# A chunked RWKV-7 recurrence on one core: odd heads keep the halves of their factors in opposite order

## The chip, the core and the metric

The program runs on one core of a Trainium2 chip. The metric is the device time of one execution in microseconds (us); lower is better. The core has a matrix engine (TensorE, PE below), a vector engine (VectorE, DVE), a scalar engine (ScalarE, ACT), GpSimd (POOL) and SyncE (SP), which here issues nearly all DMA transfers. They run at the same time and wait for each other by semaphores; each takes its own instructions in order.

## What is computed

One inference step of a decoder layer, for 2048 prompt tokens and 64 sample tokens (8 sequences of 8), in fp32 with width 1024. Token mixing has two parallel groups behind one input projection: sliding-window attention and RWKV-7 time mixing with 8 heads of 64. Then come an output projection and a gated convolutional feed-forward layer. The change touches the RWKV-7 recurrence, which the reference gives token by token:

```
def step(S, inp):
    r_t, w_t, k_t, v_t, kk_t, a_t = inp
    sa = jnp.einsum('bhij,bhj->bhi', S, kk_t)
    S = (S * w_t[:, :, None, :] - sa[..., None] * (kk_t * a_t)[:, :, None, :]
         + v_t[..., None] * k_t[:, :, None, :])
    return S, jnp.einsum('bhij,bhj->bhi', S, r_t)

S_T, ys = lax.scan(step, s0.astype(f32), xs)
```

## The kernel before

**Two kinds of work.** The dense stream (`Dense`) runs the projections P, the output projections O and the feed-forward stages F over five groups of up to 448 tokens (the last has 320). Each weight tile `w` is split into a rounded half `wh` (cast on ACT, L349) and a remainder `wl` (DVE, L350), and each product takes three float32r matmuls: `wh` with `xhi`, `wh` with `xlo`, `wl` with `xhi`. They are called gm, and pf in the second half of the feed-forward layer. The mixer (`Mixer`) runs attention and the recurrence in 8 units of 256 tokens, and one unit for the sample tokens, as generators that yield between steps.

**The recurrence in chunks.** A chunk is 64 tokens; a unit has 4, the prompt 32. The projection stage leaves for each pair of heads two factors in a DRAM tensor `ab`: `ar` (128 columns: 64 of the removal factor a, 64 of the receptance r) and `bk` (64 of b, 64 of k). Partitions 0 to 63 belong to the even head of the pair, 64 to 127 to the odd one. Per chunk:

- `scores` multiplies bk by ar into G, 128 x 128 for each head: tiles sc_e (even heads, array rows 0 to 63) and sc_o (odd heads, rows 64 to 127). A mask is applied on DVE.
- `invert` inverts the unit-triangular 64 x 64 corner of each G by 32 x 32 blocks. The diagonal blocks of a unit's heads go through DRAM (dgr) to one partition each, are inverted there by 31 steps on DVE, and come back (dxr, dtr). Two rounds of eight small matmuls (pz) join the blocks.
- `chain` walks over the chunks in order. `solve` sums into pr the part of G that acts on the values and the part of the entering state S, copies it (rhs), multiplies by the inverse (pu) and copies the result, negated, into the upper half of uv. Then pS updates S for the next chunk, and `outputs` adds state part and G part into py, which is copied to y after every second chunk.

In `solve` each head's matmul uses the same corner of the array: G's rows 64 to 127 and output partitions 0 to 63 for pr, rows 0 to 63 and the same partitions for pu.

**What sets the order.** `Clock` adds up an estimated PE time per matmul. `Flow` lets the dense stream run and, by that clock, steps the mixer's generators in windows of the dense stream; a unit may use at most its share of `UNIT` (62e3 ns) in its window. A tile framework then orders the instructions of each engine by priority and gives out buffers, so that a matmul waits for the copy that empties its buffer. The mixer has five PSUM banks: three with the tag "a" and two with the tag "o", which attention's po and the recurrence's py use.

Of the kernel before, what the change touches and what calls it, by code (L numbers as in the profile page):

```python
# [80 lines left out]
class Shared:  # L81
# [13 lines left out]
    def load(self, eng, *names):  # L95
        shapes = {"vec": [128, NV], "ident": [128, 128], "ones": [128, 128], "sel": [128, 32], "blockones": [128, 128],
                  "wkmask": [128, 128], "amask": [128, 256], "sink": [128, 8], "g_up": [96, 512], "smask": [128, 128],
                  "samask": [128, 160], "ssink": [128, 2], "sshift": [128, 14, 8], "gT": [128, 3 * KT], "cw": [128, NF, 4],
                  "sconv": [128, NF, DB, 2]}
# [8 lines left out]
    def derived(self):  # L108
# [31 lines left out]
        for i in range(2):  # L140
            s = cp.tile([128, 4, 128], F32, name=f"S{i}")
# [31 lines left out]
class Clock:  # L173
# [115 lines left out]
UNIT = 62e3  # L289
# [21 lines left out]
class Dense:  # L311
# [331 lines left out]
    def pair(self, t0, n, segs, p, k, r, vt, st):  # L643
# [58 lines left out]
        for i, t in enumerate((ar, bk)):  # L702
            self.store(sh.ab[t0 // CH:t0 // CH + m, :, p, i, :].rearrange("c q t -> q c t"), t)
# [208 lines left out]
class Mixer:  # L912
# [26 lines left out]
    def scores(self, c, mask, Gs):  # L939
# [9 lines left out]
        m = mask.unsqueeze(1).to_broadcast([128, 4, 128])  # L949
        Gv = G.rearrange("p (q e) t -> p e q t", e=2)  # L950
        for i, ps in enumerate((pe, po)):
            nc.vector.tensor_tensor(out=Gv[:, i], in0=ps.rearrange("p (q t) -> p q t", t=128), in1=m, op=ALU.mult)
# [3 lines left out]
    def invert(self, Gs):  # L956
# [4 lines left out]
        dg = self.dp.tile([64, 1024], F32, tag="dg", name="dgr")  # L961
        for c, G in enumerate(Gs):
            for b in range(2):
                q = slice(32 * b, 32 * b + 32)
                dst = dg[16 * c + 8 * b:16 * c + 8 * b + 8, :].rearrange("h (s t) -> s h t", t=32)
                nc.sync.dma_start(out=dst, in_=G[q, :, q])
# [28 lines left out]
        for c, G in enumerate(Gs):  # L995
            for b in range(2):
                q = slice(32 * b, 32 * b + 32)
                nc.sync.dma_start(out=G[q, :, q], in_=dx[16 * c + 8 * b:16 * c + 8 * b + 8, :].rearrange("h (s t) -> s h t", t=32))
# [3 lines left out]
        for c, G in enumerate(Gs):  # L1002
# [3 lines left out]
            t11 = zt[0:32].rearrange("s (h t) -> s h t", t=32)  # L1006
            pz = self.ps("pz")
            for h in range(NH):
                te.matmul(pz[32:64, 32 * h:32 * h + 32], G[0:32, h, 32:64], t11[:, h, :], start=True, stop=True)
            nc.scalar.copy(out=zt[32:64], in_=pz[32:64, 0:256])  # L1010
            yield 2500
            pz = self.ps("pz")
            for h in range(NH):
                te.matmul(pz[0:32, 32 * h:32 * h + 32], zt[32:64, 32 * h:32 * h + 32], G[32:64, h, 32:64], start=True, stop=True)
            nc.scalar.activation(out=G[0:32, :, 32:64], in_=pz[0:32, 0:256].rearrange("p (h t) -> p h t", t=32),
                                 func=AF.Copy, scale=-1.0)
            yield 1500

    def zt(self, dt, c):
        zt = self.sp.tile([64, 256], F32, tag="zt", name="zt", bufs=2)  # L1020
        self.nc.sync.dma_start(out=zt[0:32].rearrange("s (h t) -> s h t", t=32), in_=dt[16 * c:16 * c + 8, :].rearrange("h (s t) -> s h t", t=32))
# [11 lines left out]
    def solve(self, G, uv, state):  # L1033

        nc, te = self.nc, self.te
        hq = [slice(64 * h, 64 * h + 64) for h in range(NH)]
        pr = self.ps("pr")
        for h in range(NH):
            te.matmul(pr[0:64, hq[h]], G[64:128, h, 0:64], uv[64:128, hq[h]], start=h == 0, stop=False)
        for p in range(4):  # L1040
            ls = state(p)
            for i, (l, r) in enumerate(ls):
                te.matmul(pr[0:64, 128 * p:128 * p + 128], l, r, start=False, stop=p == 3 and i == len(ls) - 1)
        rhs = self.rhs("rhs")[0:64]
        nc.scalar.copy(out=rhs, in_=pr[0:64])
        yield 2500
        pu = self.ps("pu")
        for h in range(NH):
# [4 lines left out]
    def outputs(self, py, G, uv, state):  # L1053
        te = self.te
        hq = [slice(64 * h, 64 * h + 64) for h in range(NH)]
        for p in range(4):
            for i, (l, r) in enumerate(state(p)):
                te.matmul(py[:, 128 * p:128 * p + 128], l, r, start=p == 0 and i == 0, stop=False)
        for h in range(NH):
            te.matmul(py[:, hq[h]], G[:, h, 64:128], uv[:, hq[h]], start=False, stop=h == NH - 1)  # L1060

    def chain(self, c0, Gs, ys):

        nc, v, te, sh = self.nc, self.nc.vector, self.te, self.sh
        hh = [slice(0, 64), slice(64, 128)]
# [10 lines left out]
        for c in range(NC_):  # L1076
            if c % 2 == 0:
# [3 lines left out]
                for i in range(2):  # L1081
                    uvs[c + i] = self.t2("uv", tag="uv", bufs=2)
                    nc.scalar.copy(out=uvs[c + i][64:128], in_=pv[64 * i:64 * i + 64])
# [14 lines left out]
            pS4 = pS.rearrange("q (p d) -> q p d", d=128)  # L1098
            ec = sh.EC[:, c0 + c, :].unsqueeze(2).to_broadcast([128, 4, 64])
            for q in hh:  # L1100
                v.tensor_tensor(out=Sn[q, :, q], in0=pS4[q, :, q], in1=S[q, :, q], op=ALU.add)
            for q in hh:
                v.tensor_tensor(out=Sn[q, :, q], in0=Sn[q, :, q], in1=ec[q], op=ALU.mult)
            yield 500
            if c % 2 == 0:
                py = self.ps("py", "o")
            self.outputs(y_rows(py, c), G, uv, lambda p: [(ars[p][:, 64:128], S[:, p, :])])
            if c % 2 == 1:
                y = self.t2("y", tag="y", bufs=2)
                nc.scalar.copy(out=y, in_=py)  # L1110
                ys.append(y)
# [116 lines left out]
    def unit(self, u, need):  # L1228
# [10 lines left out]
        def recurrence():  # L1239
# [9 lines left out]
            if c0 + NC_ == sh.nch:  # L1249
                for q in (slice(0, 64), slice(64, 128)):  # L1250
                    self.store(a["o_wkv"][q], sh.S[self.si][q, :, q])
# [5 lines left out]
    def sample(self, need):  # L1257
# [85 lines left out]
        nc.scalar.copy(out=uv[64:128], in_=pv[0:64])  # L1343
# [3 lines left out]
        def entering(x, ps, first, last):  # L1347

            s0 = self.state(0) if x else nxt
            for p in range(4):  # L1350
                am = self.rhs("am", (DB, 64))
                v.tensor_tensor(out=am, in0=ars[p][:, x:x + 64].unsqueeze(1).to_broadcast([128, DB, 64]), in1=bm, op=ALU.mult)
                s1 = self.state(p + 1) if p < 3 else None
                yield 4000
                for b in range(DB):
                    te.matmul(ps[0:64, 128 * p:128 * p + 128], am[:, b, :], s0[:, b, :], start=first and not p and not b,
                              stop=last and p == 3 and b == DB - 1)
                s0 = s1

        pr = self.ps("pr")  # L1360
        for h in range(NH):
# [246 lines left out]
```

## Time and profile before

| | |
|---|---|
| time, median of 3 runs | 2988.53 us (2986.6 to 2989.17) |
| the profiled execution | 2993.85 us, span 2992.1 us |
| mean granted PE clock in it | 0.977 of full speed |
| PE busy | 2845.7 us, 95% |
| DVE busy | 1964.8 us, 66% |
| ACT busy | 1371.4 us, 46% |

The profile is of one execution. Busy time of PE is modelled from its pipelined matmuls, so 95% says that PE seldom idles, not that the array is full. An fp32 matmul shows as two matmuls in the trace, a float32r matmul as one.

### The profile page before, as it was taken

The page shows a single profiled execution, that of the slowest core. Times are in us where ns is not written, and L with a number is a line of the kernel's source. Part 1 is how long each engine was busy: PE and PEld are TensorE (multiplying, and loading weights), DVE is VectorE, ACT ScalarE, POOL GpSimd, SP SyncE. Part 2 cuts the span into 40 slices and gives each one's busy share as a digit, 9 for nine tenths or more (in the row PEclk, how much of TensorE's full clock was granted, in tenths as well). Part 3 has the DMA queues.
Part 4 walks back from the last instruction along what each step waited for, and adds up shares of the span by engine and source line. Part 5 has one row for each costly group of instructions (what it writes and reads, how often), then busy time and mean ns, then how long its engine had stood idle before and what let it go on. Part 6 is the DMA issues. An engine that isn't in the chain of part 4 may idle for free.

```text
span 2992.1 us, 45465 instructions
## 1 busy us (share of the span) xinstructions
PE 2845.7 (95%) x16737; PEld 2447.9 (82%) x16737; DVE 1964.8 (66%) x3862; ACT 1371.4 (46%) x2430; POOL 270.8 (9%) x531
## 2 busy tenths in 40 slices
PE   6999999989999998889999997999999999998997
PEld 4877777768878997678889885999878888997997
DVE  5787776776573546866835577455588676458566
ACT  5465453545454343555533344434455442344443
POOL 0011010000000000220100000000000011001111
PEclk9999999999999999999999998999999999999998
DMA  6675546646433345555433345433347434346443
GB/s 195 191 214 180 158 126 211 195 143 209 128 121 119 115 129 161 185 164 157 130 117 118 113 151 179 135 109 116 118 124 234 135 114 123 109 130 209 149 148 116
DMA packets 302654, 447.50 MB, mean 150 GB/s; under 512 B 94024, under 2 KB 232552, under 8 KB 302416
## 3 DMA queue, kind: packets, MB, share of 16 engines
q1 hardware_dynamic: 302000, 444.45, 47.8%
q8 instruction: 132, 2.16, 0.3%
q14 instruction: 90, 0.74, 0.1%
q10 hardware_dynamic: 432, 0.16, 0.0%
HBM read 363.18 MB, written 76.97 MB: 147 GB/s over the span
## 4 chain that ended last, share of the span: by engine, by line
PE 79%; DVE 12%; DMA 4%; ACT 2%; issue 2%; SPq 0%; DVEq 0%; POOL 0%; ACTq 0%; POOLq 0%
PE gm L182 48%; PE pf L182 15%; PE pr L182 3%; PE py L182 2%; DVE wl L350 2%; PE po L182 1%; PE pz L182 1%; PE pu L182 1%; DVE tt L984 1%; DVE tmp L983 1%; PE pS L182 1%; PE ppt L186 1%; PE sc L182 1%; PE ms L182 1%; PE sc_e L182 1%
## 5 line engine op out<-in xcount | busy, mean ns | idle before, releaser
L182 PE MATMUL gm<-xhi,wh 128*128 128x448 f32 (+3 forms) x2880 | 1059.5, 369 | 31.1 <-ACT xhi L349 17.9
L182 PE MATMUL gm<-xhi,wl 128*128 128x448 f32 (+3 forms) x2880 | 1034.8, 360 | 13.4 <-DVE wl L350 13.0
L182 PE MATMUL gm<-xlo,wh 128*128 128x448 f32 (+3 forms) x2880 | 1035.5, 360 | 3.8 <-DVE xlo L350 3.5
L349 ACT CAST wh<-w 128x1024 fp32r<-128x1024 f32 (+1 forms) x470 | 489.1, 1041 | 843.6 <-PE gm L182 413.2
L350 DVE TENSOR_TENSOR wl<-w,wh 128x1024 fp32r<-128x1024 f32 (+1 forms) x470 | 570.1, 1213 | 458.8 <-ACT wh L349 452.0
L182 PEld LDWEIGHTS gm<-xhi,wh 128*128 128x128 f32 (+2 forms) x2880 | 543.4, 189 | 119.0 <-issue 32.5
L182 PEld LDWEIGHTS gm<-xhi,wl 128*128 128x128 f32 (+2 forms) x2880 | 543.6, 189 | 68.3 <-DVE wl L350 20.3
L182 PEld LDWEIGHTS gm<-xlo,wh 128*128 128x128 f32 (+2 forms) x2880 | 544.6, 189 | 56.7 <-DVE xlo L350 11.0
L182 PE MATMUL pf<-hh,wh 128*128 128x448 f32 (+1 forms) x880 | 324.6, 369 | 13.3 <-DVE acc L856 12.0
L182 PE MATMUL pf<-hl,wh 128*128 128x448 f32 (+1 forms) x880 | 316.1, 359 | 0.0
L182 PE MATMUL pf<-hh,wl 128*128 128x448 f32 (+1 forms) x880 | 316.1, 359 | 0.0
L829 POOL COPY zcar<-zz 128x2 f32<-128x2 f32 x110 | 84.6, 769 | 1503.0 <-ACT zz L818 1503.0
L182 PEld LDWEIGHTS pf<-hh,wh 128*128 128x128 f32 x880 | 167.6, 190 | 38.4 <-DVE acc L856 15.3
L856 DVE TENSOR_TENSOR acc<-acc,pf 128x448 f32<-128x448 f32 (+1 forms) x200 | 117.6, 589 | 96.1 <-PE pf L182 94.9
L182 PEld LDWEIGHTS pf<-hh,wl 128*128 128x128 f32 x880 | 167.3, 190 | 13.4 <-issue 1.6
L182 PEld LDWEIGHTS pf<-hl,wh 128*128 128x128 f32 x880 | 167.7, 191 | 12.6 <-issue 2.5
L839 DVE TENSOR_TENSOR c<-c,gm 128x448 f32<-128x448 f32 (+1 forms) x110 | 65.2, 593 | 124.3 <-PE gm L182 107.3
L825 DVE SCALAR_TENSOR_TENSOR c<-zz,c_cw,c 128x448 f32<-128x448 f32 (+1 forms) x220 | 140.7, 640 | 8.9 <-ACT c L819 6.7
L832 ACT ACTIVATE c<-c 128x448 f32<-128x448 f32 (+1 forms) x110 | 61.2, 557 | 130.0 <-DVE c L825 97.7
L349 ACT CAST xhi<-r 128x448 fp32r<-128x448 f32 (+1 forms) x120 | 63.3, 544 | 75.7 <-DVE r L502 29.1
L983 DVE TENSOR_TENSOR tmp<-gb,tt 64x31 f32<-64x31 f32 (+21 forms) x279 | 91.6, 328 | 6.8 <-DMA gb<-dgr 4.0
L984 DVE TENSOR_TENSOR tt<-tt,tmp 64x31 f32<-64x31 f32 (+21 forms) x279 | 91.8, 329 | 2.9
(270 smaller groups left out, 3290.7 us busy)
## 6 DMA issues: line engine op xcount, KB each, us to landing
w<-in_w SPq DMA_DIRECT2D x220, 512.0 KB
w<-in_w2q SPq DMA_DIRECT2D x100, 512.0 KB
w<-in_w_all SPq DMA_DIRECT2D x90, 512.0 KB
ab<-abd SPq DMA_DIRECT2D x66, 512.0 KB
w<-in_w_out SPq DMA_DIRECT2D x40, 512.0 KB
r<-in_xT SPq DMA_DIRECT2D x64, 224.0 KB
abd<-bk SPq DMA_DIRECT2D x16, 448.0 KB
abd<-ar SPq DMA_DIRECT2D x16, 448.0 KB
```

Source lines behind the costliest of these rows:

```text
L182: return self.te.matmul(out, lhsT, rhs, **kw)
L186: return self.te.transpose(*args)
L349: self.nc.scalar.copy(out=hi, in_=src)
L350: self.nc.vector.tensor_tensor(out=lo, in0=src, in1=hi.bitcast(F32), op=ALU.subtract)
L825: v.scalar_tensor_tensor(out=c[:, :npr], in0=z[:, j:j + npr], scalar=cw(j), in1=c[:, :npr], op0=ALU.mult, op1=ALU.add)
L829: nc.gpsimd.tensor_copy(out=sh.zcar[:, f, :], in_=z[:, npr:npr + 2])
L832: nc.scalar.activation(out=c, in_=c, func=AF.Silu)
L839: v.tensor_tensor(out=c, in0=c, in1=ps, op=ALU.mult)
L856: v.tensor_tensor(out=accs[c], in0=accs[c], in1=ps, op=ALU.add)
L983: v.tensor_tensor(out=tm, in0=col, in1=row, op=ALU.mult)
L984: v.tensor_tensor(out=tt[:nb, w:, 0:w], in0=tt[:nb, w:, 0:w], in1=tm, op=ALU.subtract)
```

## The change

For odd heads the two 64-column halves of ar and of bk change places, and so do the halves of everything made from them: of G's rows and columns and of uv. The odd head's inverse then stands in rows and columns 64 to 127, the even head's in 0 to 63.

- `solve` and `outputs` alternate between the heads of a pair. For pu they use opposite corners of the array; for the G part of `solve` the even head uses rows 64 to 127 with output partitions 0 to 63, the odd one rows 0 to 63 with partitions 64 to 127.
- Both state parts, for `solve` and for `outputs`, are computed at once by one matmul per head with 64 rows and 128 output partitions, into two accumulators pc (one per parity, both with the tag "o"). pc is held until the outputs are copied.
- S holds only the diagonal blocks, 64 columns per pair, not 128. pS has one matmul per head.
- The copies rhs, uv and y, and pz's two copies, are made once for each parity.
- ab is stored with three transfers per factor in place of one; the transfers of the inversion are split by parity. The sample part loads each state half as often and without memsets.
- `Clock` counts matmuls marked `half` at half their time, and UNIT goes from 62e3 to 48e3.

```diff
-    def matmul(self, out, lhsT, rhs, **kw):
+    def matmul(self, out, lhsT, rhs, half=False, **kw):
         n = math.prod(rhs.shape[1:])
-        self.t += max(60.0, n / 2.4 * (1 if rhs.dtype == F32R else 4)) + 13.0
+        self.t += (max(60.0, n / 2.4 * (1 if rhs.dtype == F32R else 4)) + 13.0) / (2 if half else 1)
...
-UNIT = 62e3
+UNIT = 48e3
...
-            self.store(sh.ab[t0 // CH:t0 // CH + m, :, p, i, :].rearrange("c q t -> q c t"), t)
+            ab = sh.ab[t0 // CH:t0 // CH + m, :, p, i, :].rearrange("c q t -> q c t")
+            self.store(ab[0:64], t[0:64])
+            for j in range(2):
+                self.store(ab[64:128, :, 64 * j:64 * j + 64], t[64:128, :, 64 - 64 * j:128 - 64 * j])
...
             pz = self.ps("pz")
             for h in range(NH):
-                te.matmul(pz[32:64, 32 * h:32 * h + 32], G[0:32, h, 32:64], t11[:, h, :], start=True, stop=True)
-            nc.scalar.copy(out=zt[32:64], in_=pz[32:64, 0:256])
+                x, y = q[h % 2]
+                te.matmul(pz[y, hd[h // 2]], G[x, h, y], zt[x, hd[h // 2]], start=True, stop=True)
+            for x, y in q:
+                nc.scalar.copy(out=zt[y], in_=pz[y, 0:128])
...
+    def values(self, uv, pv):
+        for e in range(2):
+            self.nc.scalar.copy(out=heads(uv, e)[HH[1 - e]], in_=heads(pv, e))
+
-    def solve(self, G, uv, state):
+    def solve(self, G, uv, pc):
...
         for p in range(4):
+            d = slice(64 * p, 64 * p + 64)
+            for e, (a, k) in enumerate((HH, HH[::-1])):
+                te.matmul(pc[e][a, d], G[k, 2 * p + e, a], heads(uv, e)[k, p], half=True, start=False, stop=p == 3)
+        rhs = self.rhs("rhs")[:, 0:256]
+        for e, a in enumerate(HH):
+            nc.scalar.copy(out=rhs[a], in_=pc[e][a, 0:256])
         yield 2500
-        pu = self.ps("pu")
-        for h in range(NH):
-            te.matmul(pu[0:64, hq[h]], G[0:64, h, 0:64], rhs[:, hq[h]], start=True, stop=True)
-        nc.scalar.activation(out=uv[0:64], in_=pu[0:64], func=AF.Copy, scale=-1.0)
+        pu = self.ps("pu")[:, 0:256]
+        for p in range(4):
+            d = slice(64 * p, 64 * p + 64)
+            for e, a in enumerate(HH):
+                te.matmul(pu[a, d], G[a, 2 * p + e, a], rhs[a, d], half=True, start=True, stop=True)
+        for e, a in enumerate(HH):
+            nc.scalar.activation(out=heads(uv, e)[a], in_=pu[a].rearrange("s (p d) -> s p d", d=64), func=AF.Copy, scale=-1.0)
         yield 2500
+    def outputs(self, y, G, uv, pc):
+        for p in range(4):
+            for e, a in enumerate(HH[::-1]):
+                self.te.matmul(pc[e][a, 64 * p:64 * p + 64], G[:, 2 * p + e, a], heads(uv, e)[:, p], half=True, start=False, stop=p == 3)
+        for e, a in enumerate(HH[::-1]):
+            self.nc.scalar.copy(out=heads(y, e), in_=pc[e][a, 0:256].rearrange("s (p d) -> s p d", d=64))
...
-            yield from self.solve(G, uv, lambda p: [(ars[p][:, 0:64], S[:, p, :])])
-            pS = self.ps("pS")
+            pc = [self.ps("pc", "o") for _ in range(2)]
             for p in range(4):
-                te.matmul(pS[:, 128 * p:128 * p + 128], bkt[:, 128 * p:128 * p + 128], uv[:, 128 * p:128 * p + 128], start=True, stop=True)
...
+                for e, a in enumerate(HH):
+                    te.matmul(pc[e][:, 64 * p:64 * p + 64], ars[p][a], S[a, p, :], half=True, start=p == 0, stop=False)
+            yield from self.solve(G, uv, pc)
+            pS = self.ps("pS")[:, 0:256]
+            for p in range(4):
+                for e, a in enumerate(HH):
+                    te.matmul(pS[a, 64 * p:64 * p + 64], heads(bkt, e)[:, p], heads(uv, e)[:, p], half=True, start=True, stop=True)
+            v.tensor_tensor(out=Sn, in0=pS.rearrange("q (p d) -> q p d", d=64), in1=S, op=ALU.add)
+            v.tensor_tensor(out=Sn, in0=Sn, in1=sh.EC[:, c0 + c, :].unsqueeze(2).to_broadcast([128, 4, 64]), op=ALU.mult)
...
+        pc = [self.ps("spc", "o") for _ in range(2)]
+        s0 = nxt
+        for p in range(4):
+            am = self.b4([128, DB, 128], "am", "G")
...
+            for b in range(DB):
+                for e, x in enumerate(HH):
+                    te.matmul(pc[e][:, 64 * p:64 * p + 64], am[x, b, :], s0[x, b, :], half=True, start=not p and not b, stop=False)
+            s0 = s1
...
+            pS = self.ps("spS")
+            for e, x in enumerate(HH):
+                te.matmul(pS[x], heads(bkt, e)[:, p], um[:, :, x], half=True, start=True, stop=True)
...
+HH = [slice(0, 64), slice(64, 128)]
+def heads(t, e):
+    return t.rearrange("s (p e d) -> s e p d", e=2, d=64)[:, e]
```

The order of instructions moves with it. These are PE's rows for the first chunk of the second unit, before, from pr to pS (a row is one kind of instruction with its output tile, input tiles and output size; gm are dense matmuls):

```order
L182 MATMUL pr<-uv,G 64x64 x8
L182 MATMUL pr<-S_115,ab 64x128 x4
L182 MATMUL gm<-xhi,wl 128x448
L182 MATMUL gm<-xhi,wh 128x448
L182 MATMUL gm<-xlo,wh 128x448
...
L182 MATMUL pu<-rhs,G 64x64 x8
...
L182 MATMUL gm<-xhi,wh 128x448
L182 MATMUL pS<-uv,bkt 128x128 x4
L182 MATMUL py<-uv,G 64x64 x8
```

And the same place in the changed program:

```order
L183 MATMUL pc<-S_115,ab 128x64 x8
L183 MATMUL pc<-uv,G 64x64 x8
L183 MATMUL gm<-xhi,wh 128x448
L183 MATMUL gm<-xlo,wh 128x448
L183 MATMUL gm<-xhi,wl 128x448
L183 MATMUL pu<-rhs,G 64x64 x8
...
L183 MATMUL pS<-uv,bkt 64x64
L183 MATMUL pc<-uv,G 64x64
L183 MATMUL pS<-uv,bkt 64x64 x7
L183 MATMUL pc<-uv,G 64x64 x7
L187 MATMUL bkt<-c_ident,ab 128x128 x4
```

The state part moved ahead of the G part and stands for both pr's and py's; three dense matmuls stand between the G part and pu, where four were (the first "..." of the rows before leaves out the fourth); pS and the outputs' G part are now partly interleaved.

ACT's rows for the same chunk, before, between the copy of the values and the next chunk:

```order
L1083 COPY uv<-vt 64x512 x2
L1030 COPY bkt<-bkt 128x512
L1045 COPY rhs<-pr 64x512
L1050 ACTIVATE uv<-pu 64x512
L1030 COPY bkt<-bkt 128x512
```

And in the changed program:

```order
L1053 COPY uv<-vt 64x4x64 x4
L1047 COPY bkt<-bkt 128x512
L1064 COPY rhs<-pc 64x256 x2
L1072 ACTIVATE uv<-pu 64x4x64 x2
L1081 COPY y<-pc 64x4x64 x2
L350 CAST wh<-w 128x1024
L1047 COPY bkt<-bkt 128x512
```

Each copy became two of half the columns, and y is copied in every chunk.

## Rows read from the trace of the kernel before

**Rows 1.** The page: busy time by engine; the chain that ended last, by engine.

```profile
PE 2845.7 (95%) x16737; PEld 2447.9 (82%) x16737; DVE 1964.8 (66%) x3862; ACT 1371.4 (46%) x2430; POOL 270.8 (9%) x531
...
PE 79%; DVE 12%; DMA 4%; ACT 2%; issue 2%; SPq 0%; DVEq 0%; POOL 0%; ACTq 0%; POOLq 0%
```

**Rows 2.** Stretches: length; busy PE, PEld, DVE, ACT, POOL; granted clock; DMA.

```profile
141.00:721.00 580.00, 550.02 (x3369) 435.19 (x3368) 442.19 (x942) 296.86 (x592) 49.82 (x115) 0.97 0.60 181
721.00:1101.00 380.00, 375.90 (x2225) 328.54 (x2224) 222.34 (x407) 168.94 (x272) 29.48 (x46) 1.00 0.39 124
...
2183.00:2293.00 110.00, 105.86 (x671) 85.37 (x671) 87.28 (x196) 53.98 (x98) 0.18 (x1) 0.97 0.57 175
```

**Rows 3.** The same view for PE's matmuls of pu alone (busy, count).

```profile
141.00:721.00 580.00, 11.41 (x160) 0.97 0.60 181
...
2183.00:2293.00 110.00, 2.49 (x32) 0.97 0.57 175
```

**Rows 4.** Timeline of PE in the first unit: start, length, line, tiles, form, count.

```profile
277.74 0.69 PE L182 MATMUL pz<-zt,G 32*32 32x32 f32 x16
278.36 0.47 PE L182 MATMUL gm<-xhi,wh 128*128 128x448 f32 x1
...
295.30 1.14 PE L182 MATMUL pu<-rhs,G 64*64 64x64 f32 x16
296.37 0.47 PE L182 MATMUL gm<-xhi,wl 128*128 128x448 f32 x1
296.68 0.36 PE L182 MATMUL gm<-xhi,wh 128*128 128x448 f32 x1
296.88 0.36 PE L182 MATMUL gm<-xlo,wh 128*128 128x448 f32 x1
...
297.29 1.05 PE L182 MATMUL pS<-uv,bkt 128*128 128x128 f32 x8
298.27 1.15 PE L182 MATMUL py<-uv,G 128*64 128x64 f32 x16
...
300.77 1.14 PE L182 MATMUL pr<-uv,G 64*64 64x64 f32 x16
301.85 1.09 PE L182 MATMUL pr<-S,ab 128*64 128x128 f32 x8
302.77 1.04 PE L182 MATMUL py<-S,ab 128*64 128x128 f32 x8
```

**Rows 5.** Matmuls of pu: duration in ns (min/median/max), first and last start.

```profile
L182 PE MATMUL pu<-rhs,G x528: 218/218/267, 287.1 to 2501.3; 64*64 64x64 f32 x176
```

**Rows 6.** Timeline of PE, one scores block: first pair, last matmul.

```profile
178.28 0.37 PE L182 MATMUL sc_e<-ab 64*128 64x128 f32 x1
178.28 0.37 PE L182 MATMUL sc_o<-ab 64*128 64x128 f32 x1
...
179.17 0.27 PE L182 MATMUL sc_o<-ab 64*128 64x128 f32 x1
```

**Rows 7.** Timeline of PE, attention's po: two column halves, 512 columns.

```profile
197.11 1.08 PE L182 MATMUL po<-pT,va 128*64 128x512 f32 x4
```

**Rows 8.** ACT: the copies rhs and zt (durations in ns), the cast of wh (page).

```profile
L1045 ACT COPY rhs<-pr x32: 577/579/587, 286.2 to 2346.8; 64x512 f32<-64x512 f32 x32
...
L1010 ACT COPY zt<-pz x33: 362/363/365, 269.8 to 2481.0; 32x256 f32<-32x256 f32 x33
...
L349 ACT CAST wh<-w 128x1024 fp32r<-128x1024 f32 (+1 forms) x470 | 489.1, 1041 | 843.6 <-PE gm L182 413.2
```

**Rows 9.** SP: its longest wait (total, times, longest); issue durations of zt.

```profile
SPq L373 <- DVE wl L350: 1171.6, 344, 15.0
...
L1021 SPq DMA_DIRECT2D zt<-dtr x33: 303/318/997, 265.9 to 2476.7; - x33
```

**Rows 10.** Timeline of PE, the sample part: a state block, an spS block.

```profile
2485.76 3.71 PE L182 MATMUL pr<-st,am 128*64 128x128 f32 x32
...
2504.72 1.98 PE L182 MATMUL spS<-um,bkts 128*128 128x512 f32 x4
```

More of the change, by code (lines that the diff above doesn't have):

```diff
@@ L961, in invert, with blocks @@
         dg = self.dp.tile([64, 1024], F32, tag="dg", name="dgr")
+        def blocks(G, d, c):
+            for b in range(2):
+                for e in range(2):
+                    q, r = slice(64 * e + 32 * b, 64 * e + 32 * b + 32), 16 * c + 8 * b + 4 * e
+                    yield G[q, e::2, q], d[r:r + 4, :].rearrange("h (s t) -> s h t", t=32)
         for c, G in enumerate(Gs):
[L963 to L966, printed above, removed]
+            for x, y in blocks(G, dg, c):
+                nc.sync.dma_start(out=y, in_=x)
         yield 3000
@@ L995, in invert @@
         for c, G in enumerate(Gs):
-            for b in range(2):
-                q = slice(32 * b, 32 * b + 32)
-                nc.sync.dma_start(out=G[q, :, q], in_=dx[16 * c + 8 * b:16 * c + 8 * b + 8, :].rearrange("h (s t) -> s h t", t=32))
+            for x, y in blocks(G, dx, c):
+                nc.sync.dma_start(out=x, in_=y)
             if c < 2:
@@ L1082, in chain @@
                     uvs[c + i] = self.t2("uv", tag="uv", bufs=2)
-                    nc.scalar.copy(out=uvs[c + i][64:128], in_=pv[64 * i:64 * i + 64])
+                    self.values(uvs[c + i], pv[64 * i:64 * i + 64])
                 yield 1500
@@ L1342, in sample @@
         uv = self.t2("uvs", tag="uv", bufs=2)
-        nc.scalar.copy(out=uv[64:128], in_=pv[0:64])
+        self.values(uv, pv[0:64])
         bkt = self.bk_tok(bks, "bkts")
         yield 2500
[L1347 to L1358, printed above, removed]
@@ L1360, in sample @@
-        pr = self.ps("pr")
-        for h in range(NH):
-            te.matmul(pr[0:64, hq[h]], G[64:128, h, 0:64], uv[64:128, hq[h]], start=h == 0, stop=False)
-        yield from entering(0, pr, False, True)
-        rhs = self.rhs("rhs")[0:64]
-        nc.scalar.copy(out=rhs, in_=pr[0:64])
-        yield 2500
-        pu = self.ps("pu")
-        for h in range(NH):
-            te.matmul(pu[0:64, hq[h]], G[0:64, h, 0:64], rhs[:, hq[h]], start=True, stop=True)
-        nc.scalar.activation(out=uv[0:64], in_=pu[0:64], func=AF.Copy, scale=-1.0)
@@ L1371, in sample @@
-        py = self.ps("spy", "o")
-        yield from entering(64, py, True, False)
-        for h in range(NH):
-            te.matmul(py[0:64, hq[h]], G[:, h, 64:128], uv[:, hq[h]], start=False, stop=h == NH - 1)
-        y = self.t2("ysm", tag="y", bufs=2)
-        nc.scalar.copy(out=y[0:64], in_=py[0:64])
-        ys.append(y)
+        pc = [self.ps("spc", "o") for _ in range(2)]
+        s0 = nxt
+        for p in range(4):
+            am = self.b4([128, DB, 128], "am", "G")
+            v.tensor_tensor(out=am.rearrange("q b (j t) -> q b j t", t=64),
+                            in0=ars[p].rearrange("q (j t) -> q j t", t=64).unsqueeze(1).to_broadcast([128, DB, 2, 64]),
+                            in1=bm.unsqueeze(2).to_broadcast([128, DB, 2, 64]), op=ALU.mult)
+            s1 = self.state(p + 1) if p < 3 else None
+            yield 4000
+            for b in range(DB):
+                for e, x in enumerate(HH):
+                    te.matmul(pc[e][:, 64 * p:64 * p + 64], am[x, b, :], s0[x, b, :], half=True, start=not p and not b, stop=False)
+            s0 = s1
@@ L1379, in sample @@
+        yield from self.solve(G, uv, pc)
+        ys.append(self.t2("ysm", tag="y", bufs=2))
+        self.outputs(ys[0][0:64], G, uv, pc)
         s0 = self.state(0)
```

82 lines of the change are left out of this document (25 added, 57 removed).

## The prediction

> **What bounds the kernel now.** I read the page first: TensorE (PE) is busy 95% of the span and the chain that ended last runs 79% on PE and 12% on VectorE (DVE) [rows 1]. So a microsecond of PE work is worth about a microsecond, unless DVE is close behind. Where it is close shows in the busy time by stretches [rows 2]: 141 to 721 us (mostly projections) has DVE busy 442.19 of 580 us, 76%; 2183 to 2293 us 87.28 of 110, 79%; but 721 to 1101 us (feed-forward) only 222.34 of 380, 59%, with PE at 375.90 of 380. Counting the matmuls of pu [rows 3] places the recurrence: 160 + 32 of 528 [rows 5], 36%, lie in the two DVE-heavy stretches; the rest lies mostly where PE alone is the limit.
>
> Then the timeline of single chunks [rows 4]. A row is a block of one kind. Each fp32 matmul appears there twice, so the 8 heads of pu are 16. From the start of a block to the start of the next: pz 0.62, pu 1.07, pS 0.98, pr's first part 1.08 and its state part 0.92. py<-uv,G and py<-S,ab have the lengths of pr's parts, so I take 1.08 and 0.92 again. One chunk of 64 tokens costs, with pz twice, 1.24 + 1.07 + 0.98 + 2 x 1.08 + 2 x 0.92 = 7.29 us.
>
> **What pairs cost.** A pu block is 1.14 long and one of its matmuls 0.218 [rows 4, 5], so its 16 start (1.14 - 0.218) / 15 = 0.0615 us apart, and a tail of 1.07 - 0.92 = 0.15 is left before the next form. Two rows tell what disjoint parts of the array do. sc_e and sc_o use rows 0 to 63 and 64 to 127: they start in the same hundredth of a microsecond, and 16 need 0.89 to the last start, one pair each 0.11 after the first [rows 6]. po uses columns 0 to 63 and 64 to 127: four matmuls of 512 columns are 1.08 long [rows 7], where four of the same width on the full array are 1.98 long [rows 10]. So row halves overlap, column halves overlap, and po's two halves do it while writing one bank. Opposite corners (rows and columns both different) have no row; since either difference alone suffices, I take them as overlapping. The bounds are 1x and 2x.
>
> **The sum of the change.**
> - State part (16, of which pairs share no rows; 128 columns loaded, 64 streamed). Per pair between 0.0615 (64 and 64, pu) and 0.11 (128 and 128, sc). It loads 128 like sc, so 0.11 x 8 = 0.88, in place of 0.92 + 0.92.
> - The four 64-wide blocks G, pu, pS and outputs: 7 x 0.0615 + 0.15 = 0.58 each, 2.32 in place of 4.21.
> - pz: between 0.31 and 0.62; 0.35 twice, 0.70 in place of 1.24.
> - One more change of form per chunk, priced as the tail: 0.15.
>
> That is 4.05 for 7.29; 3.24 x 32 chunks = 104 us. The sample part: 128 state matmuls at 3.71 / 32 = 0.116 [rows 10] become 64 pairs at 0.11, 7.8 us less; spS goes from four blocks of 1.98 to four of 1.08 as po has them, 3.6 less; its own G, pu, outputs and pz, 2 less. Gross: 104 + 13 = 117 us of PE.
>
> **What is added elsewhere.** ScalarE: rhs, uv and the values are copied by head parity, two copies of 256 columns for one of 512. A 512 copy is 0.579 and a 256 copy 0.363 [rows 8], so 0.73 for 0.58; y goes from one copy of 512 in two chunks to two of 256 in each, zt and its return go from one to two (the halves cost at most the 0.363 of the whole, at least half of it). Between 0.9 and 1.6 us a chunk, 29 to 51 us on an engine busy 46% [rows 1]: free in the sum, but not in a hand-over (below). DVE: four operations on the state become two of as many columns, worth something only where DVE limits; it goes into the stretch term. SP: 228 transfers more (six for two per pair in ab, two for one in dgr, dxr and zt). I price them at nothing: SP's longest wait, 1171.6 us, is for the wl split to give a weight buffer back [rows 9], so SP sits waiting anyway; without that cover they would cost 228 x 0.318 [rows 9] = 73 us of issuing, in single file. Fewer memsets on GpSimd: it is busy 9% [rows 1], nothing. UNIT and the halved clock only decide where the mixer's steps stand among the dense matmuls; that is priced by the counts of the next part.
>
> **What is given back.** First the DVE-heavy stretches. 36% of 104 is 38 us. There gm's next weights need wh (1.04 us on ACT [rows 8]) and then wl on DVE, work that does not shrink, and the inversion's DVE steps are compressed into less time. Bounds: all 38 kept or none kept. With DVE at 76 to 79% on average, and inversion and splits arriving in bursts, I keep none. Second the hand-overs: PE computes, ACT copies twice, PE goes on. In the order of the changed program (as shown for one chunk under the change) the dense matmuls between the G block and pu, and between pu and pS, number 2 to 4 in 15 places of 64, none in 5, and 6 or more elsewhere (before, 4 or fewer in 22, among them none in 2). gm follows gm in 0.20 [rows 4], so three cover 0.6; the copies need 0.73 and the wake-up: some 0.3 x 15 + 0.9 x 5 = 9 us, plus 5 for a new hand-over, in which the next chunk's state matmuls wait for both y copies, since pc now takes both "o" buffers (six places with 3 dense matmuls or fewer, 0.8 each). Together 14 (bounds 0 and 30).
>
> Net: 117 - 38 - 14 = 65. The profiled execution took 2993.85, so the sum gives 2929 for one like it; it stood 5.3 over the median 2988.53, and 2988.53 - 65 is **2924 us**.
>
> The rows leave one rule to weigh. pu and pz put two row halves into one bank, and no row shows that. The Trainium skill (TensorEngine Tiling (Array Packing), Restrictions and Gotchas) says that different row tiles cannot access the same PSUM bank at once. po's halves share rows, so they do not test it; pc has a bank for each parity and is free of it. By the rule the sum would be that of the second rival, 2958 us; by the rows for row halves and column halves it stays 2924.
>
> **Rivals.**
> 1. Pairing as above and almost nothing given back: PE stays the only bound, and DVE's smaller load lets the heavy stretches keep their share. 117 less some 9 at the hand-overs: 2880 us. For it: PE at 95%. Against: DVE at 79%.
> 2. Opposite corners that write one bank do not overlap. Then pu loses 0.49 and both pz 0.54 a chunk, 1.03 x 33 = 34 us: 2958 us. Against it only analogy.
> 3. The changes cancel: corners and the 64-wide column halves run singly, so that only the state part gains, 0.92 + 0.92 - 0.88 - 0.15 = 0.8 x 32 = 26 us, and the 14 us of hand-overs and a third of the DVE term (13) take it back: 2988 us, no change. po speaks against it.
> 4. Slower: the y copies. The state matmuls of the next chunk stand in PE's queue with all dense matmuls behind them, and now wait for two y copies. If ACT has two casts of wh ahead (2 x 1.04 + 0.73 = 2.8, less the bkt transposes, about 0.5), PE loses 2.3 us a chunk, 74 in all: 2998 us. It decides from 65 / 32 = 2.0 us a chunk up. Before, y was copied every second chunk out of one of two buffers, so nothing waited. For it: ACT serves casts in order. Against: in most chunks 9 or more dense matmuls lie between outputs and the next state part.
>
> **How the numbers follow.** My forecast 0.60 (its own range 2900 to 2950), rival 1 0.10, rival 2 0.14, rival 3 0.06, rival 4 0.10. The predicted time is the forecast's. The range runs from 2888 to 2963: it takes in rival 2 and half of rival 1, and leaves out rivals 3 and 4 and the other half, 0.21. A measurement of this kernel can tell about 0.2%, 6 us: faster by more than that 0.60 + 0.10 + 0.14 = 0.84, same 0.06, slower 0.10.
>
> **What would show it.** In the profile after: pu's 16 matmuls starting two by two, block to next in about 0.58 (1.07 would be rival 2); the state part at 0.11 a pair; pS and outputs in 1.2 together. PE's share of the span lower than 95%, and waits of gm for ACT and DVE longer by some 40 us in all, most of them between 141 and 721 us. If instead PE's waits before the state part name ACT y, rival 4 holds. The prediction is wrong if the blocks shrink as said and the time does not follow (more is given back than the two terms), or if the blocks do not shrink.

## The result, and the profile after

The changed kernel takes 2940.64 us (median of 4, 2939.6 to 2943.48), the kernel before 2988.85 beside it: a ratio of 0.9841 [0.9824, 0.9858], 48 us less. Forecast were 2924 us in a range of 2888 to 2963. A second set of runs, further down, gave 0.9853 [0.9840, 0.9866]. The profiled execution took 2943.48 us.

The page of the kernel after, busy time by engine and the chain that ended last, answers to [rows 1]:

```profile
PE 2775.8 (94%) x16993; PEld 2358.6 (80%) x16993; DVE 1925.4 (65%) x3782; ACT 1409.3 (48%) x2644; POOL 250.9 (9%) x519
...
PE 76%; DVE 13%; DMA 4%; ACT 3%; issue 3%; SPq 1%; DVEq 0%; ACTq 0%; POOL 0%; POOLq 0%
```

Its span and mean granted TensorE clock:

```profile
core 0: 2941.7 us, clock 0.968
```

With the table of before (span 2992.1, PE busy 2845.7, clock 0.977) these lines split each span in three. **Idle** is the span less PE's busy time. **Lost to the clock** is the span times what the clock lacks of 1. The **rest** is what TensorE's work would take at full clock without a wait. The clock's third digit leaves 1.5 us open, and time in which PE idles at the lower clock stands in both columns. The other lines of the table come from the experiments.

| kernel | span | idle | lost to the clock | rest |
|---|---|---|---|---|
| before | 2992.1 | 146.4 | 68.8 | 2776.9 |
| after | 2941.7 | 165.9 | 94.1 | 2681.7 |
| after, heads not alternating | 2982.6 | 158.8 | 86.5 | 2737.3 |
| after, first unit later | 2936.4 | 163.2 | 85.2 | 2688.0 |
| before, inversion cut | 2912.0 | 103.0 | 40.8 | 2768.2 |
| after, inversion cut | 2854.3 | 122.3 | 54.2 | 2677.8 |

So TensorE's work shrank by 95 us; 20 went to more waiting and 25 to a lower granted clock, which leaves 50 between the two profiled executions. If the clock's loss is counted only where PE is busy, it is 47 us before and 68 after, and the rest shrinks from 2799 to 2708: 91 us of work, 20 of waiting, 21 of clock. How far the table can be trusted shows in the kernels without the inversion, whose matmuls are the same: their rest should not move, and it moves by 4 and 9 us, in the second way of counting by 15 and 17.

Where the work shrank shows in the timeline of PE after (start, length, line, tiles, form, count), against [rows 4]:

```profile
301.92 1.11 PE L183 MATMUL pc<-S,ab 64*128 64x64 f32 x16
302.95 0.68 PE L183 MATMUL pc<-uv,G 64*64 64x64 f32 x16
303.57 0.47 PE L183 MATMUL gm<-xhi,wh 128*128 128x448 f32 x1
...
316.42 0.69 PE L183 MATMUL pc<-uv,G 128*64 128x64 f32 x16
317.03 0.47 PE L183 MATMUL gm<-xhi,wh 128*128 128x448 f32 x1
...
687.62 0.44 PE L183 MATMUL pz<-zt,G 32*32 32x32 f32 x16
687.99 0.47 PE L183 MATMUL gm<-xhi,wh 128*128 128x448 f32 x1
...
718.24 0.68 PE L183 MATMUL pu<-rhs,G 64*64 64x64 f32 x16
718.86 0.47 PE L183 MATMUL gm<-xhi,wh 128*128 128x448 f32 x1
...
720.49 0.69 PE L183 MATMUL pS<-uv,bkt 128*64 128x64 f32 x16
721.11 0.47 PE L183 MATMUL gm<-xhi,wh 128*128 128x448 f32 x1
```

Times from a block's start to the next row: state 1.03, G 0.62, outputs 0.61, pz 0.37, pu 0.62, pS 0.62. With pz twice a chunk costs 4.24 us, where the prediction had 4.05 and before had 7.29. Single records of the pu block at 718.24 start two by two, 7 ns apart within a pair and 58 ns from pair to pair; before, single records started 58 ns apart. A record is half of an fp32 matmul.

What PE waited for after (engine, tile waited for: us in total, times, longest):

```profile
PE gm L183 <- ACT xhi L350: 20.1, 14, 7.5
PE pf L183 <- DVE acc L861: 20.1, 12, 9.2
PE gm L183 <- DVE wl L351: 15.8, 14, 4.1
...
PE pS L183 <- ACT uv L1072: 5.8, 3, 4.5
...
PE pz L183 <- DMA zt<-dtr: 2.7, 2, 2.4
...
PE pz L183 <- ACT zt L1024: 1.8, 4, 0.7
```

The same rows before:

```profile
PE gm L182 <- ACT xhi L349: 17.9, 11, 7.0
PE gm L182 <- DVE wl L350: 13.0, 13, 2.8
PE pf L182 <- DVE acc L856: 12.0, 11, 3.8
```

Before, neither pS nor pz waited for ScalarE. No matmul of pc waits for ScalarE's copies of y; only the transposes pt wait longer for the y that VectorE has normalized (4.7 us for 1.8). Of the 40 us more of waits of gm that the prediction named, 12 are there (47 before, 59 after, all rows of gm together), and 1.6 of them between 141 and 721 us on xhi and wl. The row that grew most is pf's wait for acc on VectorE, by 8 us, all of it behind 1345 us. Summed over gm and pf, the waits that name VectorE grew from 28.5 to 43.0 us.

Stretches after (length; busy PE, PEld, DVE, ACT, POOL; granted clock; DMA), against [rows 2]:

```profile
141.00:721.00 580.00, 538.89 (x3362) 412.46 (x3360) 428.86 (x921) 308.75 (x658) 56.87 (x114) 0.94 0.62 179
721.00:1101.00 380.00, 379.02 (x2446) 325.41 (x2443) 223.68 (x409) 185.71 (x325) 27.38 (x47) 1.00 0.44 138
```

Between 141 and 721 us the time hardly moved: the first gm of F0 starts at 721.5 us before and at 716.9 after. But VectorE is no busier there (428.86 us for 442.19), while the clock fell from 0.97 to 0.94. The other heavy stretch of [rows 2], 2183 to 2293 us before, became longer: the same dense matmuls lie between 2130 and 2250 us after, 120 us for 110, with the clock at 0.91 for 0.97.

```profile
2130.00:2250.00 120.00, 108.87 (x670) 85.61 (x670) 90.16 (x207) 58.06 (x118) 1.66 (x3) 0.91 0.47 148
```

### The profile page after: what moved, and what is told of

It reads as the page before. It is cut to its first block, busy times and chain, and to the rows that moved or that the text cites. A ratio compares the mean times of both kernels' runs of the same rounds, so it can differ in the third digit from the quotient of the medians.

```text
span 2941.7 us, 46311 instructions
## 1 busy us (share of the span) xinstructions
PE 2775.8 (94%) x16993; PEld 2358.6 (80%) x16993; DVE 1925.4 (65%) x3782; ACT 1409.3 (48%) x2644; POOL 250.9 (9%) x519
## 4 chain that ended last, share of the span: by engine, by line
PE 76%; DVE 13%; DMA 4%; ACT 3%; issue 3%; SPq 1%; DVEq 0%; ACTq 0%; POOL 0%; POOLq 0%
PE gm L183 47%; PE pf L183 16%; PE pc L183 2%; DVE wl L351 2%; PE po L183 1%; DVE tmp L994 1%; DVE tt L995 1%; PE pz L183 1%; PE ppt L187 1%; DMA r<-od 1%; ACT wh L350 1%; PE sc_e L183 1%; PE pu L183 1%; PE pS L183 1%; PE ms L183 1%
```

## The experiments

**The order of the heads.** In the changed kernel six kinds of block take the four even heads first and then the four odd ones.

```diff
-        for p in range(4):
-            d = slice(64 * p, 64 * p + 64)
-            for e, (a, k) in enumerate((HH, HH[::-1])):
+        for e, (a, k) in enumerate((HH, HH[::-1])):
+            for p in range(4):
+                d = slice(64 * p, 64 * p + 64)
```

> The changed kernel with the order inside six kinds of block altered (state, G, pu, pS, outputs, pz): first the four even heads, then the four odd ones, so that neighbours in TensorE's order use the same corner of the array. Copies, layout and transfers stay. If it is the neighbourhood of opposite corners that makes the blocks short, pu goes from 0.61 us to about 1.07 from its start to the next row and the state part with G from 1.65 to about 2.0 (state) + 1.07. How much of it arrives in the time tells what the pairs are worth here: if VectorE and ScalarE pace the stretches from 141 to 721 us, only the later ones lengthen, about 46 us or less, so 2975 to 2995 us; if TensorE paces everything, 90 us or more, so 3030 or more. If the corners overlap whatever their order is, or if the gain came from copies and layout, it stays within 10 us of 2941.

Measured: 2993.29 us, ratio 1.0017 [1.0005, 1.0028]. Page, clock and timeline of this kernel:

```profile
PE 2823.8 (95%) x16993; PEld 2416.6 (81%) x16993; DVE 1926.2 (65%) x3782; ACT 1412.2 (47%) x2644; POOL 251.9 (8%) x519
```

```profile
core 0: 2982.6 us, clock 0.971
```

```profile
724.99 1.60 PE L183 MATMUL pc<-S,ab 64*128 64x64 f32 x16
726.52 0.96 PE L183 MATMUL pc<-uv,G 64*64 64x64 f32 x16
...
729.46 0.96 PE L183 MATMUL pu<-rhs,G 64*64 64x64 f32 x16
730.35 0.47 PE L183 MATMUL gm<-xhi,wh 128*128 128x448 f32 x1
```

pu takes 0.89 here and 0.62 with alternating heads, the state part 1.53 and 1.03. The alternation, in all six kinds together, carries the whole gain: 52.7 us between the medians. Everything else in the change comes out 0.2% slower together, although it too takes work off TensorE (rest 2737 against 2777): its idle time and its clock loss, 30 us by the table, are those of the whole change but for 15 us. The profiled execution, 2984.33 us, was the shortest of ten, 9 us below the median, so the table flatters this kernel by some 9 us. So the shorter pairs kept nearly all that they saved (55.6 us of the rest); the losses come with the rest of the change: the copies, the layout and the new order of the program, which this run does not tell apart. The time lies at the upper end of what I gave for early stretches paced by VectorE and ScalarE, but the rows speak against that reading: the 90 us or more of the other one assumed blocks as long as before, and they are shorter (0.89 for 1.07), so the pairs had only 55.6 us to give, and 52.7 arrive.

**The planner's numbers.** UNIT back to 62e3, alone and together with full counting of the half-array matmuls.

```diff
-UNIT = 48e3
+UNIT = 62e3
```

> The changed kernel with UNIT at 62e3 as before, so that the mixer's steps are spread over the dense matmuls as if a unit were longer. If the new UNIT placed the steps badly, the time falls by 10 us or more below 2941. If waits for VectorE and ScalarE in 141 to 721 us and the lower granted clock take the gain back, the number does little: the first stretch at half clock (272 to 299 us after the change) has the same order of matmuls here, and the time stays at 2941 within 6 us.

```diff
-        self.t += (max(60.0, n / 2.4 * (1 if rhs.dtype == F32R else 4)) + 13.0) / (2 if half else 1)
+        self.t += max(60.0, n / 2.4 * (1 if rhs.dtype == F32R else 4)) + 13.0
-UNIT = 48e3
+UNIT = 62e3
```

> The changed kernel with the planner as before: UNIT 62e3, and each of the half-array matmuls counted at its full length by the planner's clock. Only the corners, copies and transfers of the change are left. If the planner's new numbers carry the loss, 2915 to 2930 us. If they carry a gain (steps placed with truer lengths), 2950 to 2960. If neither matters, 2941 within 6 us; the order still has long runs of paired matmuls without a dense one between P1 and P2, so the stretch at half clock should stay, some 20 us long or more.

Measured: 2948.07 us, 0.9862 [0.9840, 0.9885], and 2951.28 us, 0.9865 [0.9846, 0.9883]. The intervals overlap with that of the changed kernel: the new numbers are worth some 5 to 10 us at most, and they don't carry the loss. In both kernels a stretch at half clock lies between P1 and P2, as expected (274.2 to 298.1 us and 275.1 to 292.1).

**VectorE's load.** In both kernels 30 of the 31 steps of the inversion are left out, so that the inverse is not computed.

```diff
             if j and j % 4 == 0:
                 yield 1500
+            if j:
+                continue
```

> The changed kernel without 30 of the 31 steps of each inversion (the inverse is left out but for its first step), which takes some 178 us of VectorE's 1925. To be read against the same cut in the kernel before, which runs beside it. If waits for VectorE between 141 and 721 us take the gain back, the two lie 70 us apart or more. If VectorE has no part in it, they lie 45 to 55 us apart as the full kernels do. If the lower clock in long runs of short matmuls takes the gain, the distance grows only as far as the stretches at half clock go away here.

> The kernel before without 30 of the 31 steps of each inversion. Where VectorE paces the projections it comes out 30 to 100 us below 2988; if its load is hidden everywhere, within 10 us of 2988.

Measured: after 2856.46 us, 0.9570 [0.9556, 0.9584]; before 2912.42 us, 0.9753 [0.9738, 0.9767]. They lie 56 us apart, for 48 with the inversion. Their pages and clocks, before first:

```profile
PE 2809.0 (96%) x16737; PEld 2430.6 (83%) x16737; DVE 1824.6 (63%) x3322; ACT 1367.8 (47%) x2430; POOL 244.8 (8%) x531
```

```profile
core 0: 2912.0 us, clock 0.986
```

```profile
PE 2732.0 (96%) x16993; PEld 2336.7 (82%) x16993; DVE 1788.4 (63%) x3242; ACT 1406.6 (49%) x2642; POOL 233.1 (8%) x519
```

```profile
core 0: 2854.3 us, clock 0.981
```

The inversion costs both kernels dearly (76 and 84 us): VectorE's busy time falls by 140 and 137 us without it (some 178 were expected), and TensorE is held up less. Whether by VectorE's load or by the time that the inverse is waited for, this cut does not tell. But the inversion takes only 8 us more from the changed kernel. In the table the idle time grows by 19 us here too, the same as with the inversion; what is better is the clock, 13 us lost to the change in place of 25. From the first gm of P1 to the first of F0 the gain is 18 us here and 4 with the inversion.

**Where the clock falls.** The granted clock of the changed kernel has 188 us at the lower of its two levels (1.2 GHz, half of 2.4), before has 137. The longest stretch, from 272.1 to 299.4 us, has no counterpart before. It alone costs 11 to 14 us: half of the 22 us in which PE is busy in it, or half of the whole. Two others grew: 27 us in three pieces between 2214 and 2259 us, where before has 7 in the same stage, and 17 us at 504 us for 7. Stretches of the kernel after, as in [rows 2]:

```profile
262.00:269.00 7.00, 7.00 (x50) 5.51 (x48) 1.07 (x1) 1.79 (x5) 0.44 (x2) 1.00 0.40 80
269.00:276.00 7.00, 3.79 (x66) 2.44 (x64) 0.00 (x0) 1.59 (x7) 0.00 (x0) 0.72 0.25 38
276.00:283.00 7.00, 6.03 (x74) 5.06 (x76) 0.00 (x0) 4.13 (x13) 0.00 (x0) 0.50 0.91 330
283.00:290.00 7.00, 6.09 (x67) 5.15 (x68) 0.93 (x2) 3.09 (x8) 0.00 (x0) 0.50 0.77 220
290.00:297.00 7.00, 6.40 (x55) 5.09 (x54) 5.38 (x9) 4.60 (x10) 0.98 (x4) 0.50 0.35 105
```

Before, PE is busy all 7 us of each of these stretches, at full clock, as in this row of before:

```profile
283.00:290.00 7.00, 7.00 (x66) 5.89 (x63) 4.13 (x7) 3.38 (x6) 0.00 (x0) 1.00 0.86 247
```

After, no gm stands between 270.7 and 294.1 us: 218 records of pz, vt, bkt, pc, pu and pS follow each other there, the end of the first unit's inversion and its first chunks, while P2's first gm comes behind them in PE's order. They wait for each other's copies and transfers, as in this row of the same kernel's timeline (the bracket is idle time before it):

```profile
274.66 0.28 PE L183 MATMUL pz<-zt,G 32*32 32x32 f32 x2 [2.40 <-DMA zt<-dtr]
```

This longest wait began at 272.3 us, when the clock had already fallen at 272.1.

Two edits go for it. One begins the first unit half way through P1, so that its chain falls behind P2's start.

```diff
-        windows = [(f(P[1], 0), f(P[1], 1)), ...
+        windows = [(f(P[1], 0.5), f(P[1], 1)), ...
```

> The changed kernel with the first unit's window beginning half way through P1 instead of at its start. In the order the run of 115 short matmuls without a dense one between P1 and P2 is broken up (40 and 41 at the longest there), and a run of 115 stands at the end of P2 instead. If such runs, with waits inside them, are what lowers the granted clock, the stretch at half clock at 272 to 299 us goes, and one of similar length appears where P2 ends (some 420 us); the time stays within 10 us of 2941. If the clock falls at 272 us for another reason, it falls there here too.

> The kernel before with the first unit's window beginning half way through P1, as in the run of the changed kernel with the same edit. If that edit repairs something that the change brought with it (the long run of short matmuls between P1 and P2 and the half clock there), it gives the kernel before nothing: 2988 us within 5. If a later start is simply better, the kernel before gains some 9 us too: 2974 to 2982.

Measured: the changed kernel with it 2932.18 us, 0.9807 [0.9788, 0.9826]; the kernel before with it 2983.29 us, 0.9991 [0.9981, 1.0001]. Stretches of the changed kernel with it:

```profile
269.00:276.00 7.00, 7.00 (x34) 6.04 (x34) 4.59 (x10) 4.86 (x10) 1.02 (x4) 1.00 0.50 97
276.00:283.00 7.00, 7.00 (x72) 4.02 (x70) 5.76 (x10) 4.18 (x11) 0.29 (x2) 1.00 0.21 31
...
453.00:460.00 7.00, 5.46 (x80) 3.01 (x80) 0.00 (x0) 3.66 (x11) 0.00 (x0) 1.00 0.63 212
460.00:467.00 7.00, 6.08 (x64) 4.97 (x64) 0.00 (x0) 3.91 (x10) 0.00 (x0) 0.54 0.72 236
467.00:474.00 7.00, 6.55 (x72) 5.69 (x72) 1.47 (x4) 2.94 (x7) 0.06 (x1) 0.50 0.42 132
474.00:481.00 7.00, 6.61 (x56) 5.22 (x55) 5.60 (x10) 6.08 (x14) 0.86 (x4) 0.50 0.35 127
```

The half clock at 272 us is gone, and one of 20.5 us (460.5 to 481.0) stands where the long run now is, at P2's end. It follows the run. The kernel before gains nothing that can be told from no change. Its page gives the table's line:

```profile
PE 2773.2 (94%) x16993; PEld 2356.1 (80%) x16993; DVE 1925.2 (66%) x3782; ACT 1408.4 (48%) x2642; POOL 256.7 (9%) x519
```

```profile
core 0: 2936.4 us, clock 0.971
```

It is the fastest of the kernels that compute everything, 8.5 us below the changed one. By the table its loss to the clock is 9 us smaller, but that is not the moved stretch alone: 20.5 us at half clock for 27.3 is 3.4 us of loss, and the rest lies in other stretches, such as 2214 to 2259 us (17 us at half clock for 27). Its profiled execution, 2938.20 us, was the slowest of four. What the 8.5 us are made of is not shown.

The other edit puts three matmuls of 448 columns ahead of each pz, pu and pS block of the first unit; their result is overwritten.

```diff
+    def fill(self, ps):
+        if ("R", 0) not in self.done:
+            for i in range(3):
+                self.te.matmul(ps[:, 0:448], self.sh.lw[0][:, 0:128], self.sh.lw[1][:, 0:448], start=True, stop=True)
```

> The changed kernel with three extra matmuls on the full array (96 rows, 448 columns, their result is overwritten) ahead of each pz, pu and pS block of unit 0 alone: 48 of them, some 10 us of matmuls, in the stretch in which the granted clock stood at half after the change (272 to 299 us) and in which PE waits some 6 us for ScalarE and a transfer. If long runs of short paired matmuls with waits and without a dense matmul let the clock fall, that stretch at half clock goes or shrinks below 10 us, 14 us of lost clock come back, the waits are partly filled, and the time is 2930 to 2942 us in spite of the added work. If the clock falls there for another reason, the half clock stays and the time is 2946 to 2953 us.

Measured: 2954.49 us, 0.9892 [0.9874, 0.9911], and the half clock stays, from 272.8 to 293.3 us. As the kernel's timeline shows, an added matmul at the head of a block still waits for the copy that empties its buffer.

```profile
270.04 0.87 PE L183 MATMUL pz<-lw,lw 96*128 96x448 f32 x3 [0.61 <-ACT zt L1025]
270.84 0.44 PE L183 MATMUL pz<-G,zt 32*32 32x32 f32 x16
271.93 0.88 PE L183 MATMUL pz<-lw,lw 96*128 96x448 f32 x3 [0.65 <-ACT G L1033]
```

Even so most of the waits are gone: between 262 and 298 us PE waits 2.0 us here, 5.6 without the added matmuls, and the clock stands at half in a stretch in which PE is busy all the time:

```profile
283.00:290.00 7.00, 7.00 (x58) 5.73 (x57) 0.00 (x0) 3.22 (x9) 0.00 (x0) 0.50 0.67 216
```

So here neither waits nor a lack of long matmuls held the clock at half once it had fallen. What makes it fall is not settled. The kernel with the planner as before has a run of 163 short records, with 3.3 us of waits and no gm, from 441.0 to 454.7 us, and keeps full clock through it:

```profile
441.00:448.00 7.00, 5.58 (x85) 2.77 (x85) 0.00 (x0) 2.91 (x9) 0.00 (x0) 1.00 0.54 163
448.00:455.00 7.00, 5.07 (x99) 4.16 (x91) 0.40 (x1) 6.11 (x18) 0.37 (x2) 1.00 0.76 229
```

And the changed kernel without the inversion has half clock from 285.4 to 299.1 us behind a wait of 2.3 us, though no run there is longer than 36 records. So a long run is neither enough nor needed.

The changed kernel was run again beside these:

> The changed kernel once more, beside the others on one chip: 2941 us within 4, and the stretch at half clock at about 272 to 299 us again. If the clock's stretches fall elsewhere in this execution, they don't hang on the program's order and none of the readings of them stands.

Measured: 2943.41 us, 0.9853 [0.9840, 0.9866], half clock from 275.3 to 299.2 us. The stretch belongs to the program, not to one execution. The kernel with the heads not alternating has it too (271.7 to 299.0), so the alternation itself does not bring it.

**The hand-overs.** Each copy of rhs and uv in halves, so that a hand-over takes longer; then the second copy of rhs on VectorE; then more dense matmuls at the hand-overs, by longer pauses, on top of the later start.

```diff
         for e, a in enumerate(HH):
-            nc.scalar.copy(out=rhs[a], in_=pc[e][a, 0:256])
+            for j in (slice(0, 128), slice(128, 256)):
+                nc.scalar.copy(out=rhs[a, j], in_=pc[e][a, j])
```

> The changed kernel with each copy of rhs and of uv in two halves, so four copies of 128 columns where there were two of 256. A copy of 512 columns takes 0.579 us and one of 256 takes 0.363, so by the same line one of 128 would take about 0.255 (an estimate): a hand-over grows by some 0.29 us, two hand-overs in each of 33 chunks. If hand-overs stand on the path nearly everywhere, the time grows by 15 us or more, to 2956 or above; if only a third of them do, as counted in the prediction, by 5 to 8 us; if they are hidden by dense matmuls everywhere, by less than 3 us.

```diff
-        for e, a in enumerate(HH):
-            nc.scalar.copy(out=rhs[a], in_=pc[e][a, 0:256])
+        nc.scalar.copy(out=rhs[HH[0]], in_=pc[0][HH[0], 0:256])
+        nc.vector.tensor_copy(out=rhs[HH[1]], in_=pc[1][HH[1], 0:256])
```

> The changed kernel with the second of the two copies of rhs on VectorE, so that the two run side by side. If the two copies in a row hold TensorE up before pu (5.8 us of idle time before pu after the change, none before it), some 3 us come back: 2936 to 2941 us. If the copy on VectorE stands behind splits of 1.2 us, pu waits longer: 2944 to 2960 us.

```diff
-        yield 2500
+        yield 4000
```

> The changed kernel with the first unit's window beginning half way through P1, and the planner's pauses behind the copies of rhs and uv at 4000 instead of 2500, so that more dense matmuls are placed between G and pu and between pu and pS. If short cover at the hand-overs costs the time, the idle time before pu and pS goes to below 2 us and the time is 2920 to 2929 us. If not, it is that of the later start alone, 2932 us within 5, or longer where the longer chain pushes work to the end of a stage.

Measured: quarters 2949.97 us, 0.9875 [0.9854, 0.9896], beside 0.9853 for the changed kernel on the same chip; rhs on VectorE 2945.91 us, 0.9866 [0.9844, 0.9887]; longer pauses 2936.78 us, 0.9828 [0.9811, 0.9845]. The quarters cost some 7 us, in line with a third of the hand-overs on the path, but the intervals overlap: not many of them can be. Sharing the copies between engines brings nothing, and there was little to bring: the 5.8 us that the expectation names are pS's wait for uv, and pu waited 0.6 us for rhs. The longer pauses bring nothing over the later start alone either: pu waits 4.3 us for rhs in place of 5.0, but pS 2.9 for uv in place of 1.9.

## Why the prediction came out as it did

**The bound and the pairs: right.** TensorE was the bound, and opposite corners overlap. The unpaired order shows that alternation is what does it. pu's halves write one bank, and 7 ns between the two records of a pair leave no place for the second rival. The rule of the Trainium skill (TensorEngine Tiling (Array Packing), Restrictions and Gotchas), that different row tiles cannot access the same PSUM bank at once, does not hold for these blocks: a pair of records in opposite corners takes 58 ns, as long as a single record took before.

**The gross term was mis-sized: 117 us forecast, 95 measured (91 in the second way of counting).** Clean blocks are nearly as forecast: 3.05 us a chunk for 3.24, 98 us over the 32 chunks for 104. The sample part is as forecast too: busy time of its state matmuls went from 15.4 to 7.6 us and of spS from 8.1 to 4.3. What is missing lies where blocks come in pieces or woven into one another: pz stands in 94 unbroken runs where it stood in 58, pS in 64 where it stood in 32. Summed over the trace at full clock, from each record's start to the next without idle time, pz gave 8 us where the prediction had 18, pS 10 of 13, pu 14 of 16. That each piece pays the change of form, which I charged once a chunk, would explain it; no run takes it apart. On top of that the records of gm, whose number is the same, cost some 7 us more by the same count.

**The term for VectorE was the step that failed: the reason, not the size.** "With DVE at 76 to 79% on average, and inversion and splits arriving in bursts, I keep none": 38 us. Between 141 and 721 us nearly nothing was kept, but not for that reason. VectorE's share there went down, the waits for wl and xhi grew by 5 us over the whole run, and without the inversion the two kernels are only 8 us further apart. VectorE did take something, some 8 to 15 us by that run and by the waits of gm and pf that name it, but mostly between 1345 and 1850 us, outside the two stretches that the prediction had named. The loss between 141 and 721 us goes by the granted clock: 21 to 25 us in all, about 17 of them in this stretch (its clock is 0.94 after and 0.97 before, of 580 us). The other stretch, 2183 to 2293 us, even became 10 us longer, at 0.91 for 0.97. I had no term for the clock, although [rows 2] has it at 0.97 in both heavy stretches.

**The hand-overs: some 8 us for 14.** Idle time grew by 20, of which pS waiting for uv (5.8), pz for zt (1.8) and pu for rhs (0.6) are hand-overs that did not wait before. The 5 us for the state matmuls behind the y copies did not come. The copies in pieces, which cost each hand-over 0.3 us more, show some 7 us, as a third of them on the path would.

**y copies and transfers: free, as said.** No row of the waits has pc waiting for a copy of y; rival 4 did not come. Rival 1 fell because of the clock and the waits, rival 3 because the corners overlap.

Net: 95 less 20 less 25 is 50 between the profiled executions, 48 between the medians, for 65 forecast. Two errors of opposite sign hide in this: the gross term was 22 us too high, what was given back 7 us too high, and half of what was given back had a cause that the prediction did not have. That the time lies so near the forecast is in part luck: the 38 us that it took off for VectorE stand in for a clock loss that it did not see.

What stays open is why the clock falls in these stretches. Shown is that the stretch at 272 us follows the long run of short blocks when that is moved, and that it does not hang on the alternation or on the planner's numbers. But another run, of 163 records for 218, kept full clock, so the run alone does not do it, and that waits do it is only argued: with 2.0 us of them in place of 5.6 the half clock stayed.

## What to carry to other kernels

Work that uses a part of the array is worth alternating, matmul by matmul, between parts that differ in rows, in columns or in both: the same matmuls in another order were 50 us slower. When blocks shrink, split the new span into idle time, clock loss and rest before blaming a busy engine; the three come from two lines of the page, good to some 10 us here. And look at what stands in TensorE's order where a stage begins: a chain of short blocks with its own copies, without dense matmuls beside it, cost here more in clock (11 to 14 us) than in waiting (5.7), and beginning it later won 8.5 us.

## What the runs showed of the hardware

- Two records of fp32 matmuls in opposite corners of the array (64 by 64 each, two records to a matmul) cost 58 ns together, as much as a single one before, though they write one PSUM bank.
- Even without alternation TensorE reaches a little ahead. With four even heads and then four odd ones, a second series of records begins 0.29 us into a block of pu, 7 ns behind a record of the first, and the two series alternate for three more records. The records don't name their corner; that the second series is the odd heads is read from the spacing. The block takes 0.89 us, not the 1.07 of [rows 4], where all heads shared one corner.
- The granted clock stood at half for 17 to 27 us in one place of the program, in every variant of the changed kernel that had a long run of short blocks there, and 448-column matmuls put between them did not lift it: it stood at half while PE was busy 7.00 of 7.00 us. A run of 163 short records elsewhere kept full clock.
